# State tiles of four streams in the ring of raw weights, and norm sums with one column, in a one-core encoder kernel

## The chip, the core and the metric

The kernel runs on one core of a Trainium2 chip. Its time is the device time of one execution in microseconds (us); lower is better. A core has TensorE (PE; its weight loads are listed as PEld), VectorE (DVE), ScalarE (ACT), GpSimd (POOL) and SyncE (SP). All transfers of this kernel are issued from SP, in order, and run on 16 DMA engines.

## What is computed

The reference is one inference step of a layer with two mixers and an MLP, on 2048 prompt frames with 16 meta tokens ahead of them, and on 8 running streams of 16 frames each. Cut to what matters here:

```python
def rms_norm(x, g):                      # also: layer norm over the conv channels
    return x * rsqrt(mean(x * x) + EPS) * g

def retention_block(q, k, v, S):         # one chunk; S is the carried state, 128 x 128 a head
    scores = einsum('bihd,bjhd->bhij', q, k) * d_intra
    intra = einsum('bhij,bjhe->bihe', scores, v)
    inter = einsum('bihd,bhde->bihe', q, S) * d_in
    S_new = S * exp(lg * L) + einsum('bjhd,bjhe,hj->bhde', k, v, d_out)
    return intra + inter, S_new

q, k, v, gate, u = mixer_inputs(x, pos, g_pre, w_in)     # rms_norm, one projection, rotary q and k
ret = retention over chunks, conv = depthwise conv + layer norm + swish
x = x + rms_norm(concat(ret * swish(gate), conv) @ w_out)
x = x + rms_norm(relu(rms_norm(x) @ w_mlp_in) ** 2 @ w_mlp_out)
```

There are 4 heads of 128. Each of the 8 streams has a state of 128 x 128 per head, which is read, used by `inter`, updated and written back.

## The kernel before

The tokens are cut into six groups; a group is three blocks of 128 tokens, or two blocks and the 8 x 16 tokens of the streams. Group 0 also holds the meta tokens; group 3 (`SG`) holds the streams. Tokens lie in the columns of most tiles.

The first stage (up to about 1000 us) runs over the groups. For a group it normalizes x (`norm_group`), projects it with weight units of 128 x 1024 (`proj`, `values`), runs the convolution of the group on VectorE (L780), the retention of each head (`head_tail`), and one group later the output projection (`out_units`). The second stage is the MLP. Products with weights are made from operands split in a high and a low part, so each takes three matmuls (L459 to L461; L878 to L880 for values).

Weights come in through `fetch`. A unit that is met for the first time is loaded unsplit into two tiles of 128 x 512 named `raw` (a ring of five, `RB[0]`), and split by ScalarE and GpSimd (L260, L261); the split parts are saved, and from then on they are loaded in split form (`whi`, `wlo`, a ring of nine, L236 and L237). The last weight that is split before the MLP is one of `out_units` of group 1, so from then on the ring of `raw` stands idle until the first stage ends.

**A head's tail.** `head_tail` is a generator; each `yield` lets other work in. Its first step transposes k (`tk`) and makes the scores (`sc`, then `sd` on VectorE). Its second step (from L949) computes the prompt's state updates (`up`, `S`), and for group 3 the streams. For the streams, GpSimd has laid out the queries in `qdm` so that a matmul with the state of stream s reaches the columns of s only. In two rounds of four streams it makes `us` (k times v per stream, from keys masked in `ks` by VectorE and GpSimd), then twice for two streams: load the states into `sst` (L983), add their `inter` part to `os` (L985), update the states on VectorE (L987) and store them (L989). `sst` is a ring of two tiles, each for two streams. The third step makes `ob`, then for each block the mean and variance (`bn_stats`, L1001 and L1002), a reciprocal root in eight small VectorE instructions, and `on` on ScalarE (L1012), which `ot` transposes (L1017).

**Sums for norms.** `rstd_bcast` gets a tile of squares `acc`, summed over all but the partitions. It sums over the partitions with a matmul per block of 128 tokens, in which the squares are the weights and a 128 x 128 tile of ones is streamed (L432, result `st`). All 128 columns of the result are equal; column 0 is read. Then come the root, a diagonal matrix `dg` of it per block (L436), and a matmul with ones that spreads it over the partitions (`rb`, L440). It is called for the norm of each group, for the layer norm of each group's convolution (`conv_norm`, whose mean is `mu`, L799) and twice each for groups 1 and 2 ahead of the MLP (`mlp_in`).

**What sets the order.** The code is not run in the order of its text: a scheduler with a model of the times lays out each engine's instructions (`schedule_with_timeline_sim=True`), under the priorities that generators get in `advance`. A tile of a ring is reused once its last reader is done. So an edit at one place can change the order on every engine.

Of the kernel before, what the change touches and what calls it, by code (L numbers as in the profile page):

```python
# [12 lines left out]
F32 = mybir.dt.float32  # L13
# [3 lines left out]
ALU = mybir.AluOpType  # L17
# [3 lines left out]
P = 128  # L21
D_MODEL, SEQ, N_META, PAST_LEN = 1024, 2048, 16, 512
NS, SL = 8, 16
# [31 lines left out]
def _log_gamma():  # L55
    return np.log1p(-np.exp2(np.float32(-5.0) - np.arange(NH, dtype=np.float32))).astype(np.float32).astype(np.float64)
# [95 lines left out]
def build(nc, T):  # L152
    lg = _log_gamma()
    with tile.TileContext(nc, schedule_with_timeline_sim=True) as tc, ExitStack() as top:
# [26 lines left out]
        ones = cst[:, CC["ones"]:CC["ones"] + P]  # L181
# [37 lines left out]
        rawps, RB = [], [5]  # L219
# [190 lines left out]
        def rsqrt_small(ss, nb, n):  # L410
            return rsqrt(ss, n, *(spool.tile([P, 4], F32, tag=f"nw{i}", name=f"nw{i}")[:, :nb] for i in range(5)))
# [12 lines left out]
        def rstd_bcast(acc, W, n):  # L424

            starts = list(range(0, W - P + 1, P))
            if starts[-1] + P < W:
                starts.append(W - P)
            nb = len(starts)
            ps = auxp.tile([P, 4, P], F32, tag="aux", name="st")  # L430
            for b, s in enumerate(starts):
                nc.tensor.matmul(ps[:, b, :], acc[:, s:s + P], ones, start=True, stop=True)  # L432
            y = rsqrt_small(ps[:, :nb, 0], nb, n)
            dg = spool.tile([P, NM // P, P], F32, tag="dg", name="dg", bufs=1)
            for b in range(nb):
                nc.vector.tensor_scalar(out=dg[:, b, :], in0=ident, scalar1=y[:, b:b + 1], scalar2=None, op0=ALU.mult)  # L436
            yield WAIT
            rb = auxp.tile([P, 512], F32, tag="aux", name="rb")
            for b, s in enumerate(starts):
                nc.tensor.matmul(rb[:, s:s + P], ones, dg[:, b, :], start=True, stop=True)  # L440
            return rb[:, :W]
# [39 lines left out]
        def mlp_in(gi):  # L481
# [27 lines left out]
            def norm(acc):  # L509
                if early:  # L510
                    rb = yield from rstd_bcast(acc, N, D_MODEL)
                    rs = tp.tile([P, WM], F32, tag="rs", name="rs", bufs=1)[:, :N]
                    nc.scalar.activation(out=rs, in_=rb, func=AF.Copy)
                    return rs
                sb = np_.tile([P, WM], F32, tag="acc", name="acc")[:, :N]
                nc.scalar.activation(out=sb, in_=acc, func=AF.Copy)
                yield WAIT
                return (yield from rstd_wide(sb, N, D_MODEL))
# [114 lines left out]
        tp = em(tc.tile_pool(name="tp", bufs=2))  # L633
# [15 lines left out]
        qdm = stp.tile([P, NS * P], F32, name="qdm")  # L649
# [3 lines left out]
        def norm_group(gi):  # L653
# [27 lines left out]
            for k in range(KT):  # L681
                add_square(acc[:, :W], xk[k], k, W, eng=nc.gpsimd if gi == 1 else None)
                yield
            yield WAIT
            rb = yield from rstd_bcast(acc[:, :W], W, D_MODEL)
            if gi == 0:
                rs = tp.tile([P, WM], F32, tag="rs", name="rs", bufs=1)
# [102 lines left out]
        def conv_norm(gi):  # L790
            N = LAY[gi]["N"]
            z = [zs[gi, c] for c in range(4)]
            acc = np_.tile([P, WM], F32, tag="acc", name="cacc")[:, :N]
            nc.vector.tensor_tensor(out=acc, in0=z[0][:, :N], in1=z[1][:, :N], op=ALU.add)
            nc.vector.tensor_tensor(out=acc, in0=acc, in1=z[2][:, :N], op=ALU.add)
            nc.vector.tensor_tensor(out=acc, in0=acc, in1=z[3][:, :N], op=ALU.add)
            yield WAIT
            mu = auxp.tile([P, 512], F32, tag="aux", name="mu")
            nc.tensor.matmul(mu[:, :N], ones, acc, start=True, stop=True)  # L799
            acc2 = np_.tile([P, WM], F32, tag="acc", name="cacc2")[:, :N]  # L800
            for c in range(4):
                nc.vector.scalar_tensor_tensor(out=z[c][:, :N], in0=mu[:, :N], scalar=-1.0 / (4 * P),
                                               in1=z[c][:, :N], op0=ALU.mult, op1=ALU.add)
                add_square(acc2, z[c][:, :N], c, N, 4 * P)
            yield WAIT
            rb = yield from rstd_bcast(acc2, N, 4 * P)
            for c in range(4):
                nc.vector.tensor_tensor(out=z[c][:, :N], in0=z[c][:, :N], in1=rb, op=ALU.mult)
                sg = tp.tile([P, WM], F32, tag="sg", name="csg")
                nc.scalar.activation(out=sg[:, :N], in_=z[c][:, :N], func=AF.Sigmoid, scale=pcol("cln_g", c),  # L810
                                     bias=pcol("cln_b", c))
                nc.vector.tensor_scalar(out=z[c][:, :N], in0=z[c][:, :N], scalar1=pcol("cln_g", c),
                                        scalar2=pcol("cln_b", c), op0=ALU.mult, op1=ALU.add)
                e1 = nc.vector if c < 3 else nc.gpsimd
                e1.tensor_tensor(out=z[c][:, :N], in0=z[c][:, :N], in1=sg[:, :N], op=ALU.mult)
                split(z[c][:, :N], cats[gi][0][:, 4 + c, :N], cats[gi][1][:, 4 + c, :N])
                yield
            normed.add(gi)
# [85 lines left out]
        def head_tail(gi, h, kr, qr, vf):  # L904
            g = LAY[gi]
            m, N, nb, smp = g["meta"], g["N"], g["nb"], g["smp"]
            nt = nb + smp
            blk = [slice(b * P, (b + 1) * P) for b in range(nt)]
            sblk = slice(nb * P, N)

            tk = auxp.tile([P, 512], F32, tag="aux", name="tk")
            tv = auxp.tile([P, 512], F32, tag="aux", name="tv") if m else None
# [19 lines left out]
            for b in range(nt):  # L932
# [5 lines left out]
                                    in1=dmask[:, h, :].unsqueeze(1).to_broadcast([P, nt, P]), op=ALU.mult)  # L938
            nc.gpsimd.tensor_tensor(out=v3(qd, nb), in0=v3(qr, nb),
                                    in1=din[:, h, :].unsqueeze(1).to_broadcast([P, nb, P]), op=ALU.mult)  # L940
            if smp:
# [3 lines left out]
                                        in0=qr[:, sblk].rearrange("p (s x) -> p s x", s=NS),  # L945
                                        in1=din[:, h, :SL].unsqueeze(1).to_broadcast([P, NS, SL]), op=ALU.mult)
# [11 lines left out]
            for b in range(nb):  # L958
# [3 lines left out]
                else:  # L962
                    sn = stp.tile([P, P], F32, tag=f"S{h}", name=f"S{h}", bufs=2)
                nc.vector.scalar_tensor_tensor(out=sn, in0=S[h], scalar=float(np.exp(lg[h] * P)), in1=up[:, blk[b]],
                                               op0=ALU.mult, op1=ALU.add)
# [3 lines left out]
            if smp:  # L969
                osm = auxp.tile([P, 512], F32, tag="aux", name="os")[:, :P]  # L970
                for s0 in range(0, NS, 4):
                    us = auxp.tile([P, 4, P], F32, tag="aux", name="us")
                    for s in (s0, s0 + 2):
                        ks = tp.tile([P, 2, P], F32, tag="ks", name="ks")
                        eng = nc.vector if s % 4 < 1 else nc.gpsimd
                        eng.tensor_tensor(out=ks, in0=kd[:, sblk].unsqueeze(1).to_broadcast([P, 2, P]),
                                          in1=smask[:, s:s + 2].unsqueeze(2).to_broadcast([P, 2, P]), op=ALU.mult)
                        for i in range(2):
                            nc.tensor.matmul(us[:, s - s0 + i], ks[:, i], vt[:, sblk], start=True, stop=True)
                    for s1 in (0, 2):  # L980
                        s = s0 + s1
                        sst = tp.tile([P, 2, P], F32, tag="sst", name="sst", bufs=2)
                        nc.sync.dma_start(sst, T["state"][h][:, s:s + 2, :])  # L983
                        for i in range(2):
                            nc.tensor.matmul(osm, qdm[:, (s + i) * (P - SL):(s + i) * (P - SL) + P], sst[:, i],  # L985
                                             start=(s + i == 0), stop=False)
                        nc.vector.scalar_tensor_tensor(out=sst, in0=sst, scalar=float(np.exp(lg[h] * SL)),  # L987
                                                       in1=us[:, s1:s1 + 2], op0=ALU.mult, op1=ALU.add)
                        nc.sync.dma_start(T["o_ss"][h][:, s:s + 2, :], sst)  # L989
                nc.tensor.matmul(osm, sd[:, sblk], vt[:, sblk], start=False, stop=True)  # L990
            yield

# [7 lines left out]
            for b in range(nt):  # L1000
# [7 lines left out]
                                           op1=ALU.mult)  # L1008
# [368 lines left out]
```

## Time and profile before

| what | value |
|---|---|
| median of the 3 runs shown | 2451.93 us |
| range of these runs | 2447.64 to 2454.78 us |
| the profiled execution, its own time | 2451.31 us |
| its span, first to last instruction | 2449.4 us |
| TensorE busy | 2358.0 us (96%) |
| VectorE busy | 1512.6 us (62%) |
| ScalarE / GpSimd busy | 913.3 / 1135.8 us |
| mean granted clock of TensorE | 0.982 |
| HBM | 445.20 MB read, 136.61 MB written |

Busy times are shares of the whole span, over stages with different limits. A matmul's listed duration is its latency; matmuls overlap, so spacing is read from the starts of neighbours. The granted clock is 1 at 2.4 GHz and 0.5 at 1.2 GHz; a value between is a mean over a stretch. A fp32 matmul counts as two passes in the trace, each with a weight load of its own.

### The profile page before, as it was taken

To read this page: it belongs to the slowest core of one execution; us is meant where nothing else is said; L and a number is where in the kernel's file an instruction comes from. 1 tells how busy PE (TensorE), PEld (TensorE's weight loads), DVE (VectorE), ACT (ScalarE), POOL (GpSimd) and SP (SyncE) were. 2 spreads that over 40 slices of the span, in tenths; PEclk is the share of its full clock that TensorE was granted. 3 is DMA by queue.
4 is the path that set the end of the run, shared out by engine and by line. 5 is a ranking of instruction groups with operands and counts; after the bars stand their busy time and mean duration, and the time that the engine had idled before them with its cause. 6 is when DMAs were issued, how large, how long until landed. Compare 5 with 4: busy or idle time off the path is not lost.

```text
span 2449.4 us, 40812 instructions
## 1 busy us (share of the span) xinstructions
PE 2358.0 (96%) x14538; PEld 2328.0 (95%) x14538; DVE 1512.6 (62%) x3320; ACT 913.3 (37%) x1928; POOL 1135.8 (46%) x1028
## 2 busy tenths in 40 slices
PE   7999999997999998899999999999999999999997
PEld 7898999997999998899999999999999999999996
DVE  8999896996987956456643347465433375333335
ACT  5544334133233234444444444333222353333332
POOL 6846232132132115778797785333522355332333
PEclk9999999998999999899999999999999999999998
DMA  8887787897687779658796567676854477555552
GB/s 312 294 312 274 258 293 253 253 346 255 202 299 256 251 238 351 217 204 306 268 325 206 185 226 234 233 232 225 287 168 148 157 235 252 181 175 187 179 183 86
DMA packets 246332, 584.53 MB, mean 239 GB/s; under 512 B 31984, under 2 KB 106480, under 8 KB 246128
## 3 DMA queue, kind: packets, MB, share of 16 engines
q1 hardware_dynamic: 246128, 581.92, 70.1%
q8 instruction: 115, 1.88, 0.3%
q14 instruction: 89, 0.73, 0.1%
HBM read 445.20 MB, written 136.61 MB: 238 GB/s over the span
## 4 chain that ended last, share of the span: by engine, by line
PE 71%; DVE 13%; DMA 9%; issue 3%; POOL 2%; ACT 1%; SPq 0%; DVEq 0%; POOLq 0%; ACTq 0%
PE mm L1171 8%; PE mm L1172 7%; PE mm L1173 7%; PE mm L459 5%; PE mm L461 5%; PE mm L460 5%; PE mma L459 4%; PE mma L460 4%; PE mma L461 4%; PE mmc L460 4%; PE mmc L461 4%; PE mmc L459 4%; DVE cv L780 4%; DMA s<-yscr 3%; PE mm L878 1%
## 5 line engine op out<-in xcount | busy, mean ns | idle before, releaser
L261 POOL TENSOR_TENSOR wlo<-raw,whi 128x512 fp32r<-128x512 f32 x276 | 362.7, 1334 | 283.1 <-PE mma L461 113.2
L1173 PE MATMUL mm<-op,wp 128*128 128x384 f32 (+1 forms) x1344 | 440.4, 329 | 4.6 <-POOL wp L300 4.5
L1172 PE MATMUL mm<-op,wp 128*128 128x384 f32 (+1 forms) x1344 | 441.7, 329 | 2.7 <-DVE op L329 2.7
L1171 PE MATMUL mm<-op,wp 128*128 128x384 f32 (+1 forms) x1344 | 438.9, 329 | 4.7 <-DMA wp<-wprod 2.3
L780 DVE SCALAR_TENSOR_TENSOR cv<-ext,par,cv 128x384 f32<-128x384 f32 (+1 forms) x720 | 381.4, 569 | 2.0
L459 PE MATMUL mm<-hhi,whi 128*128 128x384 f32 (+2 forms) x992 | 333.5, 336 | 18.5 <-ACT whi L260 7.0
L461 PE MATMUL mm<-hhi,wlo 128*128 128x384 f32 (+2 forms) x992 | 332.0, 336 | 5.9 <-DVE wlo L261 2.7
L460 PE MATMUL mm<-hlo,whi 128*128 128x384 f32 (+2 forms) x992 | 331.5, 335 | 0.3
L1233 DVE TENSOR_TENSOR ya<-mmc,ya 128x384 f32<-128x384 f32 (+1 forms) x344 | 182.3, 535 | 210.2 <-PE mmc L461 208.8
L1233 DVE TENSOR_TENSOR ya<-mma,ya 128x384 f32<-128x384 f32 (+1 forms) x344 | 182.8, 534 | 197.5 <-PE mma L461 196.7
L329 POOL TENSOR_TENSOR fl<-c,fh 128x384 fp32r<-128x384 f32 (+1 forms) x144 | 142.4, 989 | 335.8 <-ACT fh L328 306.2
L459 PE MATMUL mma<-fh,whi 128*128 128x384 f32 (+1 forms) x768 | 254.1, 332 | 6.9 <-DVE ya L1233 5.8
L1171 PEld LDWEIGHTS mm<-op,wp 128*128 128x128 f32 x1344 | 253.4, 189 | 7.7 <-DMA wp<-wprod 3.5
L1173 PEld LDWEIGHTS mm<-op,wp 128*128 128x128 f32 x1344 | 254.1, 189 | 5.4 <-POOL wp L300 5.2
L1172 PEld LDWEIGHTS mm<-op,wp 128*128 128x128 f32 x1344 | 254.1, 189 | 3.8 <-DVE op L329 3.3
L459 PE MATMUL mmc<-fh,whi 128*128 128x384 f32 (+1 forms) x768 | 251.1, 328 | 2.6 <-ACT fh L328 2.6
L460 PE MATMUL mma<-fl,whi 128*128 128x384 f32 (+1 forms) x768 | 251.7, 328 | 0.8 <-POOL fl L329 0.8
L460 PE MATMUL mmc<-fl,whi 128*128 128x384 f32 (+1 forms) x768 | 251.8, 328 | 0.6 <-POOL fl L329 0.6
L461 PE MATMUL mmc<-fh,wlo 128*128 128x384 f32 (+1 forms) x768 | 251.2, 328 | 1.0 <-POOL wlo L261 1.0
L461 PE MATMUL mma<-fh,wlo 128*128 128x384 f32 (+1 forms) x768 | 251.7, 328 | 0.4 <-POOL wlo L261 0.4
L260 ACT ACTIVATE whi<-raw 128x512 fp32r<-128x512 f32 x288 | 167.7, 623 | 153.0 <-PE mm L1173 83.1
L459 PEld LDWEIGHTS mm<-hhi,whi 128*128 128x128 f32 x992 | 191.8, 193 | 21.3 <-ACT whi L260 8.2
(234 smaller groups left out, 4872.2 us busy)
## 6 DMA issues: line engine op xcount, KB each, us to landing
wp<-wprod SPq DMA_DIRECT2D x224, 512.0 KB, 4.1
raw<-w SPq DMA_DIRECT2D x256, 256.0 KB, 3.8
wprod<-wp SPq DMA_DIRECT2D x112, 512.0 KB, 3.8
whi<-wkeep_in SPq DMA_DIRECT2D x108, 512.0 KB, 6.3
wlo<-wkeep_in SPq DMA_DIRECT2D x108, 512.0 KB, 5.4
raw<-w_in SPq DMA_DIRECT2D x72, 256.0 KB, 5.4
whi<-wkeep_out SPq DMA_DIRECT2D x36, 512.0 KB, 6.3
wlo<-wkeep_out SPq DMA_DIRECT2D x36, 512.0 KB, 5.6
```

The costliest lines, as they stand in the source:

```text
L260: nc.scalar.activation(out=hi[:, c], in_=raw, func=AF.Copy)
L261: (nc.vector if i < 24 and i % 4 == 0 else nc.gpsimd).tensor_tensor(out=lo[:, c], in0=raw, in1=hi[:, c].bitcast(F32), op=ALU.subtract)
L329: (eng or nc.gpsimd).tensor_tensor(out=lo, in0=src, in1=hi.bitcast(F32), op=ALU.subtract)
L459: nc.tensor.matmul(ps, whi(k), ahi(k), start=(k == 0), stop=False)
L460: nc.tensor.matmul(ps, whi(k), alo(k), start=False, stop=False)
L461: nc.tensor.matmul(ps, wlo(k), ahi(k), start=False, stop=(k == nk - 1))
L780: nc.vector.scalar_tensor_tensor(out=o, in0=src(t), scalar=wt, in1=o, op0=ALU.mult, op1=ALU.add)
L878: nc.tensor.matmul(o, hhi[:, k, c], whi, start=(k == 0), stop=False)
L1171: nc.tensor.matmul(ps, hi, ops[:, k, :n], start=start, stop=False, skip_group_check=not first)
L1172: nc.tensor.matmul(ps, hi, ops[:, 4 + k, :n], start=False, stop=False, skip_group_check=not first)
L1173: nc.tensor.matmul(ps, lo, ops[:, k, :n], start=False, stop=(k == 3), skip_group_check=not first)
L1233: last_y[0] = nc.vector.tensor_tensor(out=y, in0=ps, in1=y, op=ALU.add)
```

## The change

Two edits. First, `head_tail` of group 3 takes two tiles from the ring of `raw` at its start, each for four streams, and issues their loads there; four streams are then used, updated by one VectorE instruction and stored by one transfer. Second, the sums over the partitions in `rstd_bcast` stream one column of ones and write one column.

```diff
@@ rstd_bcast
-                nc.tensor.matmul(ps[:, b, :], acc[:, s:s + P], ones, start=True, stop=True)
+                nc.tensor.matmul(ps[:, b, :1], acc[:, s:s + P], ones[:, :1], start=True, stop=True)
@@ head_tail, start
+            ssts = []
+            for s0 in range(0, NS if smp else 0, 4):
+
+                ssts.append(rawps[0].tile([P, 512], F32, tag="raw", name="sst", bufs=RB[0]).rearrange(
+                    "p (s d) -> p s d", s=4))
+                nc.sync.dma_start(ssts[-1], T["state"][h][:, s0:s0 + 4, :])
@@ head_tail, streams
-                    for s1 in (0, 2):
-                        s = s0 + s1
-                        sst = tp.tile([P, 2, P], F32, tag="sst", name="sst", bufs=2)
-                        nc.sync.dma_start(sst, T["state"][h][:, s:s + 2, :])
-                        for i in range(2):
-                            nc.tensor.matmul(osm, qdm[:, (s + i) * (P - SL):(s + i) * (P - SL) + P], sst[:, i],
-                                             start=(s + i == 0), stop=False)
-                        nc.vector.scalar_tensor_tensor(out=sst, in0=sst, scalar=float(np.exp(lg[h] * SL)),
-                                                       in1=us[:, s1:s1 + 2], op0=ALU.mult, op1=ALU.add)
-                        nc.sync.dma_start(T["o_ss"][h][:, s:s + 2, :], sst)
+                    sst = ssts[s0 // 4]
+                    for i in range(4):
+                        nc.tensor.matmul(osm, qdm[:, (s0 + i) * (P - SL):(s0 + i) * (P - SL) + P], sst[:, i],
+                                         start=(s0 + i == 0), stop=False)
+                    nc.vector.scalar_tensor_tensor(out=sst, in0=sst, scalar=float(np.exp(lg[h] * SL)), in1=us,
+                                                   op0=ALU.mult, op1=ALU.add)
+                    nc.sync.dma_start(T["o_ss"][h][:, s0:s0 + 4, :], sst)
```

In the changed kernel, lines behind `head_tail`'s start have numbers six higher, and lines behind the streams' part three higher (the loads are L915, `os` L988, the store L992, `ot` L1020).

Where instructions now stand, at two places. Row texts are those of the schedule: line, operation, tile<-tiles, shape, and the semaphores that the row waits for (DMAHW are those of transfers).

The transfer queue (SP) in head 1 of group 3, before: stores of the first two `sst` tiles (6873, 6879), and behind them the loads of the next two (6894, 6900).

```order
L537 DMA hd0_108<-s_6816 128x384 [waits DMAHW4_49,DVE_49]
L989 DMA o_ss<-sst_6873 128x256 [waits DMAHW5_49,DVE_49]
L989 DMA o_ss<-sst_6879 128x256 [waits DMAHW6_49,DVE_49]
L537 DMA hd0_108<-s_6921 128x384 [waits DMAHW7_49,DVE_49]
L237 DMA wlo_7479<-wkeep_in_96 128x1024 [waits DMAHW0_49,PE_49]
L236 DMA whi_7559<-wkeep_in_96 128x1024 [waits DMAHW1_49,PE_49]
L983 DMA sst_6894<-state 128x256 [waits DMAHW5_49,DMAHW2_49]
L983 DMA sst_6900<-state 128x256 [waits DMAHW6_49,DMAHW3_49]
L237 DMA wlo_7560<-wkeep_in_96 128x1024 [waits DMAHW4_49,PE_49]
L236 DMA whi_7602<-wkeep_in_96 128x1024 [waits PE_49]
```

SP in the changed kernel, during `out_units` of group 1: the first three of eight state loads (6055 and 6057 for head 0, 6779 for head 1), between the last `raw` loads and saves of split weights.

```order
L259 DMA raw_4531<-w_out 128x512 [waits DMAHW0_49,Pool_49]
L322 DMA wkeep_out_97<-wlo_4294 128x1024 [waits DMAHW1_49,Pool_49]
L915 DMA sst_6055<-state 128x512 [waits DMAHW2_49]
L237 DMA wlo_4380<-wkeep_out_97 128x1024 [waits DMAHW3_49,PE_49]
L1042 DMA yscr1_100<-yo_4266 128x384 [waits DMAHW4_49,Activation_49]
L320 DMA wkeep_out_97<-whi_4429 128x1024 [waits DMAHW5_49,Activation_49]
L236 DMA whi_4489<-wkeep_out_97 128x1024 [waits DMAHW6_49,PE_49]
L1042 DMA yscr1_100<-yo_4330 128x384 [waits DMAHW7_49,Activation_49]
L915 DMA sst_6057<-state 128x512 [waits DMAHW0_49,Pool_49]
L322 DMA wkeep_out_97<-wlo_4430 128x1024 [waits DMAHW1_49,Pool_49]
L915 DMA sst_6779<-state 128x512 [waits DMAHW2_49]
L237 DMA wlo_4490<-wkeep_out_97 128x1024 [waits DMAHW3_49,PE_49]
```

The fourth and fifth follow within ten rows. The loads moved from group 3 into group 1's output projection, two groups earlier; the sixth to eighth stand in group 3, each behind the store that frees its tile. The last of them, for head 3 (7348), stands as follows in head 1 of group 3, behind the store of 6779:

```order
L992 DMA o_ss<-sst_6779 128x512 [waits DMAHW6_49,DVE_49]
L537 DMA hd0_108<-s_6743 128x384 [waits DMAHW7_49,DVE_49]
L537 DMA hd0_108<-s_6812 128x384 [waits DMAHW0_49,DVE_49]
L992 DMA o_ss<-sst_6781 128x512 [waits DMAHW1_49,DVE_49]
L237 DMA wlo_7368<-wkeep_in_96 128x1024 [waits DMAHW2_49,PE_49]
L236 DMA whi_7446<-wkeep_in_96 128x1024 [waits DMAHW3_49,PE_49]
L537 DMA hd0_108<-s_6905 128x384 [waits DMAHW4_49,DVE_49]
L915 DMA sst_7348<-state 128x512 [waits DMAHW6_49,DMAHW5_49]
L702 DMA cos_7442<-cos 128x384 [waits DVE_49]
```

TensorE (PE) in group 3, before: the end of head 1's streams has just passed; `mu`, `ot` and `st` follow one another, then head 2's `tk` and `sc`, then a projection.

```order
L461 MATMUL mm_7563<-hhi_5346,wlo_7388 128x384
L799 MATMUL mu_7062<-cacc_6991,cst_91 128x384 [waits DVE_49]
L1017 MATMUL ot_7106<-cst_91,on_7058 128x128 [waits Activation_49]
L1017 MATMUL ot_7106<-cst_91,on_7058 128x128
L1017 MATMUL ot_7106<-cst_91,on_7058 128x128 [waits Activation_49]
L432 MATMUL st_7115<-cst_91,cacc2_7064 128x128 [waits DVE_49]
L432 MATMUL st_7115<-cst_91,cacc2_7064 128x128 x2
L914 MATMUL tk_7172<-cst_91,kr_6852 128x128 x3
L933 MATMUL sc_7179<-qr_6957,kr_6852 128x128 [waits Activation_49]
L933 MATMUL sc_7179<-qr_6957,kr_6852 128x128 x2
L459 MATMUL mm_7606<-hhi_5346,whi_7478 128x384 [waits DMAHW0_49,DVE_49]
```

PE in the changed kernel, head 1's streams: both halves of `os` now stand right behind the first `us`.

```order
L985 MATMUL us_6860<-vt_5732,ks_6861 128x128 [waits DVE_49]
L985 MATMUL us_6860<-vt_5732,ks_6861 128x128
L985 MATMUL us_6860<-vt_5732,ks_6865 128x128 [waits Pool_49]
L985 MATMUL us_6860<-vt_5732,ks_6865 128x128
L988 MATMUL os_6859<-sst_6779,qdm_126 128x128 x4
L988 MATMUL os_6859<-sst_6781,qdm_126 128x128 x4
L993 MATMUL os_6859<-vt_5732,sd_6794 128x128 [waits Pool_49]
L460 MATMUL mm_7213<-hlo_3630,whi_6985 128x384
```

`mu` follows 30 rows later, 102 rows earlier than before, and after it 55 projections' matmuls. Then:

```order
L1020 MATMUL ot_7090<-cst_91,on_7042 128x128 [waits Activation_49]
L459 MATMUL mm_7450<-hhi_5346,whi_7284 128x384
L1020 MATMUL ot_7090<-cst_91,on_7042 128x128 [waits Activation_49]
L432 MATMUL st_7099<-cst_91,cacc2_7048 128x1 [waits DVE_49]
L1020 MATMUL ot_7090<-cst_91,on_7042 128x128 [waits Activation_49]
L432 MATMUL st_7099<-cst_91,cacc2_7048 128x1 x2
L920 MATMUL tk_7160<-cst_91,kr_6848 128x128 x3
L460 MATMUL mm_7450<-hlo_5347,whi_7284 128x384
```

Before, nothing stood between `mu` and `ot`, or between `st` and the next projection's wait but head 2's `tk` and `sc`; now projections stand ahead of `ot`, between `tk` and `sc` (20), and behind `sc`.

## Rows read from the trace of the kernel before

**Rows 1.** the page, part 1: busy time of the engines

```profile
PE 2358.0 (96%) x14538; PEld 2328.0 (95%) x14538; DVE 1512.6 (62%) x3320; ACT 913.3 (37%) x1928; POOL 1135.8 (46%) x1028
```

**Rows 2.** the page, part 4: the chain that ended last, by engine

```profile
PE 71%; DVE 13%; DMA 9%; issue 3%; POOL 2%; ACT 1%; SPq 0%; DVEq 0%; POOLq 0%; ACTq 0%
```

**Rows 3.** windows: length, busy PE, PEld, DVE, ACT, POOL, clock, DMA share, GB/s

```profile
500.00:600.00 100.00, 90.47 (x559) 88.41 (x559) 79.91 (x218) 30.28 (x69) 28.72 (x31) 0.93 0.88 306
600.00:700.00 100.00, 93.66 (x601) 92.68 (x600) 94.58 (x223) 26.19 (x58) 22.11 (x23) 0.98 0.69 229
1200.00:1400.00 200.00, 200.00 (x1154) 199.73 (x1153) 82.39 (x151) 85.19 (x163) 164.90 (x139) 1.00 0.70 243
```

**Rows 4.** timeline of PE: start, us, line, tiles, count [idle before <-releaser]

```profile
541.31 0.38 PE L878 MATMUL mm<-whi,hhi 128*128 128x256 f32 x1 [1.86 <-DVE kr L826]
562.88 1.06 PE L985 MATMUL os<-sst,qdm 128*128 128x128 f32 x8
585.01 0.82 PE L1017 MATMUL ot<-cst,on 128*128 128x128 f32 x3 [1.90 <-ACT on L1012]
587.69 1.65 PE L432 MATMUL st<-cst,cacc 128*128 128x128 f32 x6 [1.85 <-DVE cacc L454]
594.50 0.69 PE L459 MATMUL mm<-hhi,whi 128*128 128x384 f32 x1 [3.24 <-DVE gs L898]
603.50 1.16 PE L985 MATMUL os<-sst,qdm 128*128 128x128 f32 x8 [0.51 <-DVE S L964]
605.45 1.13 PE L979 MATMUL us<-vt,ks 128*128 128x128 f32 x8 [0.79 <-DVE z L808]
611.70 1.51 PE L985 MATMUL os<-sst,qdm 128*128 128x128 f32 x8 [4.04 <-DMA sst<-state]
```

**Rows 5.** waits, 480 to 660: total us, times, longest us

```profile
DVE sst L987 <- PE os L985: 10.8, 4, 8.3
PE os L985 <- DMA sst<-state: 5.7, 3, 4.0
```

**Rows 6.** timeline of the transfer queue: start, us, line, transfer

```profile
567.68 1.62 SPq L989 DMA_DIRECT2D o_ss<-sst  x2
573.30 0.81 SPq L983 DMA_DIRECT2D sst<-state  x2
```

**Rows 7.** tile sst: time from issue to landing

```profile
DMA to landing us min/median/max: 2.1/4.2/10.2
```

**Rows 8.** timeline of DVE, 553 to 580

```profile
560.08 0.81 DVE L796 TENSOR_TENSOR cacc<-cacc,z 128x384 f32<-128x384 f32 x1
579.57 0.42 DVE L987 SCALAR_TENSOR_TENSOR sst<-sst,us 128x256 f32<-128x256 f32 x1 [8.28 <-PE os L985]
```

**Rows 9.** windows of 10 us

```profile
580.00:590.00 10.00, 6.25 (x31) 5.19 (x31) 6.14 (x21) 3.36 (x8) 1.76 (x2) 0.77 0.82 283
590.00:600.00 10.00, 6.76 (x26) 6.46 (x26) 7.45 (x23) 6.97 (x16) 1.34 (x2) 0.55 0.36 111
610.00:620.00 10.00, 8.30 (x42) 8.20 (x43) 8.23 (x22) 2.78 (x8) 4.63 (x6) 0.83 0.26 81
```

**Rows 10.** tile st: ns min/median/max, first and last start, forms

```profile
L432 PEld LDWEIGHTS st<-cst,acc x60: 187/192/193, 13.3 to 734.5; 128*128 128x128 f32 x60
L432 PE MATMUL st<-cst,acc x60: 269/275/276, 13.4 to 734.6; 128*128 128x128 f32 x60
L432 PE MATMUL st<-cst,cacc x34: 271/275/580, 173.1 to 905.1; 128*128 128x128 f32 x34
```

**Rows 11.** timeline of PE at 13 us

```profile
13.40 0.83 PE L432 MATMUL st<-cst,acc 128*128 128x128 f32 x6
```

**Rows 12.** timeline of PE at 723 us

```profile
722.74 1.65 PE L953 MATMUL up<-vt,kd 128*128 128x128 f32 x6 [3.35 <-DVE sd L937]
```

**Rows 13.** timeline of PE at 220 us

```profile
219.93 0.54 PE L459 MATMUL mm<-hhi,whi 128*128 128x384 f32 x1 [1.85 <-DMA whi<-wkeep_in]
222.29 0.69 PE L461 MATMUL mm<-hhi,wlo 128*128 128x384 f32 x1 [1.50 <-DMA wlo<-wkeep_in]
```

## The prediction

> **What bounds the kernel now.** I read the page first. TensorE is busy for 96% of the span [rows 1] and 71% of the chain that ended last lies on it [rows 2]. So time comes back in two ways only: TensorE is given less to do, or it waits less. For the waits I went to the stretch that the change touches. The four head tails of group 3 (the group with the stream blocks) run from 498 to 643 us. In the two windows of 100 us there TensorE is idle for 9.5 and 6.3 us, and VectorE is nearly as full as TensorE, above all from 600 to 700 [rows 3]. The timeline of TensorE names the pauses: 1.86 before a value matmul, 1.90 before `ot`, 1.85 before `st`, 3.24 before a gate's projection, 0.51 and 0.79 in head 2's tail and 4.04 before `os` [rows 4].
>
> The list of waits ties them to the state tiles. TensorE waited 5.7 us in three places for a state to land, and VectorE waited 10.8 us in four places for `os`, because its update of a state (L987) stands in its in-order queue until `os` has read that state [rows 5]. The queue of transfers shows why a state is late: the `sst` ring has two tiles, so a load stands behind the store of the tile before it. In head 1 the store is issued at 567.68 and the load at 573.30 [rows 6]; a transfer of `sst` or `o_ss` takes 4.2 us to land in the middle, 10.2 at most [rows 7]. So head 1's second half of `os` runs just ahead of 579.57, where VectorE's wait of 8.28 us for it ends, though the sum that `mu` needs (`cacc`) was done by 560.9 [rows 8]. Behind that wait come the bn statistics, `on` and `ot`, then `mu`, `cacc2`, `st`, and after them the squares and the gate that free the bank for the next projection. These are the pauses from 585 to 605. They also cost clock: the granted clock is 0.77 of full in 580 to 590, 0.55 in 590 to 600 and 0.83 in 610 to 620 [rows 9], that is, after each longer pause TensorE ran for a time at the lower of its levels, 1.2 in place of 2.4 GHz.
>
> **The change, part by part.**
>
> *State loads.* Sixteen loads and sixteen stores of 128 KB become eight and eight of 256 KB; the bytes stay. The queue's rows show five loads issued already among the output weights of group 1, two groups before use; the sixth to eighth wait for the stores of the first to third. Both halves of `os` in head 1 now stand right behind `us`, where the first half ran at 562.88 [rows 4].
>
> - Waits for a state: 5.7 us [rows 5]. I take all of it. Bounds: nothing comes back if the late three loads are again late; at most 5.7.
> - Clock lost behind the 4.04 pause: TensorE was busy 8.30 us of 610 to 620 at 0.83 [rows 9], so 8.30 x 0.17 = 1.4. All of it goes with the pause.
> - The chain behind head 1's late `os`: pauses 1.90 + 1.85 + 3.24 + 0.51 + 0.79 = 8.3 [rows 4], and clock 6.25 x 0.23 + 6.76 x 0.45 = 1.4 + 3.0 = 4.4 [rows 9], together 12.7. The new order has `mu` 102 instructions earlier on TensorE and 55 projections between it and the first `ot`, where none stood before; at 0.173 us each (1154 matmuls of that width fill 200 us of the MLP [rows 3]) this is 9.5 us of cover. Against the whole coming back: the gate's pause comes from a crowd on VectorE, of which the state wait is only a part. I take two thirds, 8.5; bounds 0 and 12.7.
> - VectorE: sixteen updates of 128x256 become eight of 128x512, the same elements with half the starts. Nothing.
> - The 1.86 pause before a value matmul [rows 4] comes from the rotary step and stays.
>
> *Raw ring.* Its five tiles now carry state from the last split weight of group 1 on. Until the MLP no weight is split, so nothing else asks for them. Five times 256 KB more are loaded during group 1's output projection, where TensorE has none of the pauses above. Nothing, while the weights' lead covers it.
>
> *Sums with one column.* 60 + 34 = 94 passes of 128 columns [rows 10] (47 matmuls, two passes each). Six in a row take 0.83 us from the first's start to the last's end, each 0.275 long: (0.83 - 0.275) / 5 = 0.111 us a pass [rows 10, 11]. The trace has no pass with one column. Free passes would save 94 x 0.111 = 10.4; a pass still limited by loading its 128 weight columns saves nothing. Each pass has a load of 0.19 us [rows 10], and nothing in the trace that loads 128 columns follows its forerunner closer than 0.111. That is the nearest row, so I take 1.0; bounds 0 and 10.4, and below 0 under the rivals.
>
> The Trainium skill speaks here against the change: "TensorE: Matmul & The Clock Gate", section "LDWEIGHTS (loading the stationary operand)", has a load take the number of its columns over 1.2 ns, 107 ns for 128; by that an estimate of the saving is 94 x 0.004 = 0.4 us. The same page's section "Back-to-back issue gap" has a matmul of 1 to 64 columns follow after 25 ns; by that it would be 94 x 0.086 = 8 us. The trace can't part the two, since streaming 128 columns in two steps each takes the same 0.111.
>
> *A new order.* The scheduler lays out the stage up to about 1000 us anew on every engine; the MLP's rows read almost as before. Other small pauses will be hit or missed, each of the size of the ones seen (0.5 to 1.9). I charge 2 us.
>
> Sum: 5.7 + 1.4 + 8.5 + 1.0 - 2 = 14.6. The profiled execution took 2451.3 us (span 2449.4), 0.6 under the median of the runs shown, 2451.9, so either may be the base. 2451.3 - 14.6 = 2436.7: I predict **2437 us**. A measurement of this kernel can tell about 0.3%, 7.4 us, from no change.
>
> **The rivals.**
>
> 1. *VectorE was the bound there anyway.* TensorE arrives earlier and waits for VectorE instead. For: VectorE is busy 94.6 of 100 us from 600 to 700 [rows 3]; the pause before `up` at 722.74 (3.35, for `sd` of VectorE) is of that kind [rows 12], and the new order has the same pattern there. Against: VectorE gets back its own 10.8 us of waits. Then about half of the first three terms stays, 7.8 - 2 + 1 = 6.8, less a pause like 3.35: 2445 to 2450.
> 2. *Weights come late.* The queue of transfers is in order; the late loads stand in it until stores land, and weights stand behind them. That is what the pauses of 1.85 and 1.50 at 219.93 and 222.29 look like [rows 13], with 1.4 to 3.0 of lost clock behind such pauses [rows 9]: 5 us a time. Three would eat the gain: 2451. Against: a weight is asked for three units ahead, 3 x 24 matmuls x 0.173 = 12 us, and a store lands in about 4 [rows 7].
> 3. *Slower: loads that nothing hides.* With one column nothing streams while the next weights load. If each pass then paid its load and its own latency in full, 0.19 + 0.275 = 0.467 in place of 0.111 [rows 10, 11], that is 94 x 0.356 = 33 us. The rest gives 13.6, so 2471. It comes out slower by more than 0.3% from a spacing of 0.111 + (13.6 + 7.4) / 94 = 0.334 us a pass. Against: loads run ahead of the passes everywhere else (0.19 long at a spacing of 0.111).
> 4. *The loads are not early.* The queue's rows exclude this for five of eight.
>
> **How the numbers follow.** Forecast 0.70 (2427 to 2444: the chain term from 1 to its bound of 12.7, the sums from 0 to some 8); rival 1 0.14; rival 2 0.08, of which 0.02 ends slower; rival 3 0.08. So faster 0.70, same 0.20 (0.14 + 0.06), slower 0.10. The range goes from 2427 to 2452, which takes in rivals 1 and 2; rival 3 and a gain above 24 us stay outside.
>
> **What would show it.** Right: in group 3 no wait of TensorE for `sst`, VectorE's wait for `os` under 3 us in all, no granted clock under 0.9 in the windows that answer to 580 to 620, TensorE's idle time there (15.8 us in 500 to 700) down to about 5. For the sums: the spacing of the one-column passes; 0.1 confirms the load as limit, 0.03 would add 7 us of gain. Wrong: the pauses come back under other names between 560 and 730, weights named as releasers at 320 to 360 or 560 to 620, or `st` passes over 0.2 apart.

## The result, and the profile after

The changed kernel takes 2424.22 us (median of 4 runs, 2420.58 to 2427.17), the kernel before 2453.36 in runs beside it: a ratio of 0.9881 (95% interval 0.9869 to 0.9893), 29.1 us less. The forecast was 14.6 less, 2437, and the range ended at 2427. The direction was right, the size half of what came. The profiled execution of the changed kernel took 2426.03 us, 25.2 less by its span.

The page, part 1 [rows 1]:

```profile
PE 2346.8 (97%) x14538; PEld 2319.5 (96%) x14538; DVE 1507.9 (62%) x3312; ACT 913.9 (38%) x1928; POOL 1138.5 (47%) x1028
```

TensorE does the same 14538 passes in 11.2 us less busy time (a pass at the lower clock is busy for longer), and the rest of the gain, 14.0 us of the span, is idle time. The windows that answer to [rows 3] and, in tens, to [rows 9], in the same columns:

```profile
500.00:600.00 100.00, 96.98 (x642) 95.26 (x641) 91.78 (x238) 38.67 (x86) 37.52 (x38) 1.00 0.91 322
600.00:700.00 100.00, 100.00 (x645) 99.93 (x644) 93.69 (x228) 24.81 (x56) 24.04 (x25) 1.00 0.78 265
...
580.00:590.00 10.00, 10.00 (x68) 10.00 (x67) 10.00 (x27) 6.28 (x15) 3.29 (x3) 1.00 0.82 271
590.00:600.00 10.00, 8.34 (x62) 8.12 (x61) 10.00 (x15) 6.24 (x14) 6.48 (x6) 1.00 0.62 201
```

Idle time of TensorE in 500 to 700 went from 15.8 to 3.0 us, and no window is below full clock. VectorE is fuller than before from 500 to 600 (91.8 against 79.9 us) and about as full after it, yet between 494 and 678 us TensorE's waits for it come to 2.9 us in place of 8.3. The timeline of TensorE, where [rows 4] were:

```profile
558.98 1.95 PE L988 MATMUL os<-sst,qdm 128*128 128x128 f32 x16
560.77 0.39 PE L993 MATMUL os<-vt,sd 128*128 128x128 f32 x2
...
566.61 0.81 PE L799 MATMUL mu<-cacc,cst 128*128 128x384 f32 x2
...
576.78 0.27 PE L1020 MATMUL ot<-cst,on 128*128 128x128 f32 x1
...
577.17 0.28 PE L432 MATMUL st<-cst,cacc 128*128 128x1 f32 x2
...
596.73 0.55 PE L920 MATMUL tk<-cst,kr 128*128 128x128 f32 x3 [1.66 <-DVE sst L990]
```

All of head 1's `os` is done by 561.2; `mu` comes at 566.61 (582.30 before), and `ot` and `st` follow 10 us later with projections between and no pause. All that TensorE waited for in group 3 (494 to 678 us):

```profile
PE tk L920 <- DVE sst L990: 1.7, 1, 1.7
PE ob L998 <- DVE sst L990: 0.7, 1, 0.7
PE rb L440 <- DVE dg L436: 0.5, 1, 0.5
```

The two new waits are for the update of a state (L990), which now takes 683 ns in one piece. The queue's row shows the loads of the states:

```profile
L915 SPq DMA_DIRECT2D sst<-state x8: 332/424/773, 327.5 to 568.0; - x8
L990 DVE SCALAR_TENSOR_TENSOR sst<-sst,us x8: 672/683/689, 509.4 to 620.1; 128x512 f32<-128x512 f32 x8
```

**Where the gain lies.** Four marks on TensorE cut the trace: `tk` of head 0 in group 3, the first `tk` of group 4, the last `mu` (the convolution of the last group), and the first `sw` (a norm inside the MLP). Before:

```profile
493.32 0.49 PE L914 MATMUL tk<-cst,kr 128*128 128x128 f32 x3
697.84 0.49 PE L914 MATMUL tk<-cst,kr 128*128 128x128 f32 x3
895.74 0.81 PE L799 MATMUL mu<-cacc,cst 128*128 128x384 f32 x2
1085.33 0.81 PE L418 MATMUL sw<-acc,cst 128*128 128x384 f32 x2
```

After:

```profile
494.40 0.49 PE L920 MATMUL tk<-cst,kr 128*128 128x128 f32 x3
678.03 0.49 PE L920 MATMUL tk<-cst,kr 128*128 128x128 f32 x3
873.73 0.81 PE L799 MATMUL mu<-cacc,cst 128*128 128x384 f32 x2
1056.81 0.81 PE L418 MATMUL sw<-acc,cst 128*128 128x384 f32 x2
```

Group 3 went from 204.5 to 183.6 us (20.9 less), groups 4 and 5 from 197.9 to 195.7, the entry of the MLP from 189.6 to 183.1 (6.5 less), a stretch that neither edit touches. What comes ahead costs 1.1 more and the rest of the MLP some 3 more. So two things had to be explained: why group 3 gave more than the 15.6 forecast for it, and why the MLP's entry gave anything.

### The profile page after: what moved, and what is told of

Same layout as the page of the kernel before. It is cut to its first block, busy times and chain, and to the rows that moved or that the text cites. A ratio compares the mean times of both kernels' runs of the same rounds, so it can differ in the third digit from the quotient of the medians.

```text
span 2424.2 us, 40779 instructions
## 1 busy us (share of the span) xinstructions
PE 2346.8 (97%) x14538; PEld 2319.5 (96%) x14538; DVE 1507.9 (62%) x3312; ACT 913.9 (38%) x1928; POOL 1138.5 (47%) x1028
## 4 chain that ended last, share of the span: by engine, by line
PE 72%; DVE 10%; DMA 10%; POOL 3%; issue 2%; ACT 1%; SPq 1%; DVEq 0%; POOLq 0%; ACTq 0%
PE mm L1174 7%; PE mm L1175 7%; PE mm L1176 7%; PE mm L461 6%; PE mm L460 6%; PE mm L459 6%; PE mmc L460 4%; PE mma L459 4%; PE mmc L461 4%; PE mma L460 4%; PE mmc L459 4%; PE mma L461 4%; DVE cv L780 3%; DMA s<-yscr 3%; DMA st<-hd 2%
## 5 line engine op out<-in xcount | busy, mean ns | idle before, releaser
L1236 DVE TENSOR_TENSOR ya<-mma,ya 128x384 f32<-128x384 f32 (+1 forms) x344 | 182.9, 534 | 196.5 <-PE mma L461 195.7
```

Of the source, the lines that this page charges most:

```text
L1236: last_y[0] = nc.vector.tensor_tensor(out=y, in0=ps, in1=y, op=ALU.add)
```

## The experiments

Three theories. **A**: a state that is there when `os` wants it gives back its wait and the whole chain behind it; that is the gain in group 3. **C**: the one-column sums give some 10 us. **B**, later sharpened to **L**: part of the gain comes from the layout, not from the states' times. The state tiles left the pool `tp`, which became 2 KB a partition smaller; when the MLP's pools are laid over the first stage's, other tiles come to lie on each other (read from the code; no run shows the addresses).

All eleven kernels by the marks of their own traces (one profiled execution each, so good to a few us; the ratios are from the timed runs; the trace with `tp` as large as before is of the longest of its six executions, 2440.84 us against a median of 2432.95, and it reaches group 3 some 4 us later than the changed kernel's):

| kernel | ratio to before | group 3 | groups 4, 5 | MLP's entry |
|---|---|---|---|---|
| before | 1 | 204.5 | 197.9 | 189.6 |
| changed | 0.9881 (0.9869 to 0.9893) | 183.6 | 195.7 | 183.1 |
| states alone | 0.9865 (0.9852 to 0.9879) | 185.1 | 195.7 | 179.5 |
| sums alone | 1.000 (0.9987 to 1.0013) | 205.6 | 195.1 | 191.4 |
| one late tile of four | 0.9951 (0.9935 to 0.9967) | 213.1 | 184.2 | 179.4 |
| two tiles of four | 0.9868 (0.985 to 0.9886) | 183.3 | 194.7 | 180.1 |
| changed, `tp` as large as before | 0.992 (0.9905 to 0.9935) | 184.4 | 198.2 | 190.2 |
| before, `tp` smaller | 0.9963 (0.995 to 0.9976) | 204.3 | 198.2 | 181.4 |
| updates in pairs | 0.9877 (0.9862 to 0.9892) | 184.0 | 194.8 | 181.2 |
| `stq` ahead of `x1p` | 0.9966 (0.9953 to 0.9979) | 185.5 | 197.1 | 198.8 |
| `stq` of four tiles | 0.9882 (0.9861 to 0.9904) | 183.4 | 196.2 | 182.9 |

**1. The states alone** (the change without its second edit):

```diff
-                nc.tensor.matmul(ps[:, b, :1], acc[:, s:s + P], ones[:, :1], start=True, stop=True)
+                nc.tensor.matmul(ps[:, b, :], acc[:, s:s + P], ones, start=True, stop=True)
```

> The state part of the change alone: states of four streams early in the raw ring, the sums with 128 columns as before. Its laid-out order is nearly that of the changed kernel. Theory A (the states and the chain behind them give the gain; one column saves (0.111 - 0.094) x 94 = 1.6 us at most): 2424 to 2427. Theory C (the one-column sums give some 10 us of it): 2432 to 2435. Theory B (part of the gain is the new order): 2424 to 2427 too, since the order is kept.

Measured: 2422.05. The first edit brings the whole gain. It makes the states early and `tp` smaller at once; runs 5 and 6 part the two.

**2. The sums alone** (the kernel before with the second edit).

> The sums part alone: one column streamed and written in rstd_bcast, the states in pairs in a ring of two as before. Its laid-out order is nearly that of the kernel before. Theory A: 2450 to 2453 (0 to 1.6 us gained, group 3 with its waits for sst, the MLP's entry as before). Theory C: 2443. If the one-column sums bring the shorter entry of the MLP, the stretch from 900 to 1060 us is some 9 us shorter here.

Measured: 2453.87 against 2453.46. Theory C falls: one column brings nothing, within 0.13%. Group 3 and the MLP's entry are as before.

**3. One late tile.** All states go through one tile of four streams, so a load stands behind the store of the round before (the loads at the head's start are gone):

```diff
-                    sst = ssts[s0 // 4]
+                    if not held:
+                        held.append(rawps[0].tile([P, 512], F32, tag="raw", name="sst", bufs=RB[0]).rearrange(
+                            "p (s d) -> p s d", s=4))
+                    sst = held[0]
+                    nc.sync.dma_start(sst, T["state"][h][:, s0:s0 + 4, :])
```

> The changed kernel, but all states go through one tile of four streams, loaded in the round that uses it, so that each load stands behind the store of the round before, as in a ring of two pairs. Theory A: the waits for sst come back and with them the chain in group 3: 15 to 25 us lost there, 2440 to 2450. Theory B (the gain comes from the new order and from the fewer, larger instructions): 2424 to 2432, the waits for sst covered by other work. The MLP's entry tells whether its 9 us hang on early states.

Measured: 2440.52, as theory A has it. Groups 3 to 5 together take 397.2 us, against 379.3 in the changed kernel: 18 us that come with late states. (The two are taken together, since group 3 is longer here than before the change and groups 4 and 5 shorter.) What TensorE waited for in group 3 is the lesson of this run:

```profile
PE sc L934 <- ACT rn L1021: 4.8, 1, 4.8
PE ot L1019 <- ACT on L1014: 3.9, 1, 3.9
PE rb L440 <- DVE dg L436: 2.7, 1, 2.7
...
PE os L987 <- DMA sst<-state: 1.1, 1, 1.1
```

and VectorE, in the same stretch:

```profile
DVE sst L989 <- PE os L987: 8.3, 2, 7.8
```

The wait that names the state is 1.1 us. The other 11.4 listed here are under the names of ScalarE and VectorE: VectorE's queue holds an update that waits for `os`, and ScalarE's `on` behind it waited for VectorE's `nm`. That each of these waits goes back to a late state is read from the order of the queues; no run parts them. The MLP's entry is short here too, though the states are late: it doesn't hang on them.

**4. Two tiles of four**, held for the whole group, loaded a head ahead:

```diff
-                ssts.append(rawps[0].tile([P, 512], F32, tag="raw", name="sst", bufs=RB[0]).rearrange(
-                    "p (s d) -> p s d", s=4))
+                if len(held) < 2:
+                    held.append(rawps[0].tile([P, 512], F32, tag="raw", name="sst", bufs=RB[0]).rearrange(
+                        "p (s d) -> p s d", s=4))
+                ssts.append(held[(2 * h + s0 // 4) % 2])
```

> The changed kernel, but with two fixed tiles of four streams in place of the ring of five: the loads of a head stand behind the stores of the head before it, some 25 us before their use. Theory A (a state must be there when os wants it, and no earlier): 2422 to 2428, no wait of TensorE for sst. If the depth of five is what counts: 2432 or more, with waits for sst in group 3.

Measured: 2423.63. A ring of two tiles of four does all that the ring of five does: heads 1 to 3 are loaded within group 3, so loads two groups ahead are not needed for them.

**5. The changed kernel with `tp` as large as before.** An unused tile takes the place that the states had left:

```diff
+            if smp and h == 0:
+                pad = tp.tile([P, 2, P], F32, tag="pad", name="pad", bufs=2)
+                nc.gpsimd.memset(pad[:, 0, :1], 0.0)
```

> The changed kernel, with an unused tile of 2 KB a partition put into the pool that the pairs of states had left, so that this pool is as large as before; states early as in the change. Laid out so, the transfers at the MLP's entry stand in the order of before again. Theory L (some 6 to 10 us of the gain come from the smaller pool, because the MLP's tiles that are loaded first lie over the tiles of the first stage): from the last mu to the first sw 189 to 192 us in place of 179 to 183, 2430 to 2434 in all; group 3 as fast as in the changed kernel (20 us ahead of before at head 0's tk of group 4). Theory A alone (all of the gain is early states): 2421 to 2426.

Measured: 2432.95; the entry is 190.2, group 3 stays at 184.4. Theory L holds. What TensorE waited for between the last `mu` and the first `sw` (longest rows; `wp` is a part of an MLP weight made from `raw`, `op` and `chi` are parts of split operands), here:

```profile
PE mm L1179 <- POOL wp L300: 3.3, 2, 2.7
PE mm L461 <- DMA wlo<-wkeep_out: 3.0, 2, 2.5
PE mm L1178 <- DVE op L329: 2.4, 2, 1.8
```

in the kernel before:

```profile
PE mm L1173 <- POOL wp L300: 4.5, 1, 4.5
PE mm L461 <- DMA wlo<-wkeep_out: 3.9, 1, 3.9
PE mm L1172 <- DVE op L329: 2.7, 2, 1.9
```

and in the changed kernel:

```profile
PE mm L459 <- ACT chi L328: 3.8, 2, 3.5
PE mm L461 <- DMA wlo<-wkeep_out: 2.8, 1, 2.8
PE mm L1176 <- POOL wp L300: 1.5, 1, 1.5
```

The pad brings back the waits of before, line by line (L1173 and L1179 are the same line). The queue of transfers shows another order as well. With the pad the MLP's raw weights come one, then three (L282; the tiles into which h is loaded, L561, are called `st` as well):

```profile
917.96 0.33 SPq L282 DMA_DIRECT2D raw<-w  x1
...
930.94 2.96 SPq L282 DMA_DIRECT2D raw<-w  x3
```

as in the kernel before:

```profile
932.12 0.33 SPq L282 DMA_DIRECT2D raw<-w  x1
...
946.51 2.89 SPq L282 DMA_DIRECT2D raw<-w  x3
```

and in the changed kernel two, behind seven loads of h:

```profile
901.96 14.96 SPq L561 DMA_DIRECT2D st<-hd  x7
917.02 0.85 SPq L282 DMA_DIRECT2D raw<-w  x2
```

**6. The kernel before with the smaller `tp`.** Its two tiles of two streams are the halves of one raw tile, and everything else is as before:

```diff
-                        sst = tp.tile([P, 2, P], F32, tag="sst", name="sst", bufs=2)
+                        if not held:
+                            held.append(rawps[0].tile([P, 512], F32, tag="raw", name="sst", bufs=RB[0]).rearrange(
+                                "p (s d) -> p s d", s=4))
+                        sst = held[0][:, s1:s1 + 2]
```

> The kernel before, with its two state tiles of two streams cut from one tile of the raw ring: the rhythm of loads, updates and stores as before, only the pool of the stage's tiles is 2 KB smaller. Theory L: group 3 as slow as before, the MLP's entry 6 to 10 us shorter, 2443 to 2447. Theory A alone: 2450 to 2455.

Measured: 2442.91. Group 3 is as slow as before, the entry as short as after, with the changed kernel's longest waits there (`wlo` 3.1, `chi` 2.9, `wp` 1.5 us) and its order of transfers (two raw weights behind seven loads of h). With run 5 this closes a square: early states alone give 0.80%, the layout alone 0.37%, together 1.17%; both at once measured 1.19%. Of 2453.4 us that is 19.6 and 9.1. Within the intervals, which are 0.13 to 0.15% either way, the two gains are separate and add up (run 5 has the one-column sums as well, which run 2 puts at nothing).

**7. Updates and stores in pairs**, states early:

```diff
-                    nc.vector.scalar_tensor_tensor(out=sst, in0=sst, scalar=float(np.exp(lg[h] * SL)), in1=us,
-                                                   op0=ALU.mult, op1=ALU.add)
-                    nc.sync.dma_start(T["o_ss"][h][:, s0:s0 + 4, :], sst)
+                    for s1 in (0, 2):
+                        nc.vector.scalar_tensor_tensor(out=sst[:, s1:s1 + 2], in0=sst[:, s1:s1 + 2],
+                                                       scalar=float(np.exp(lg[h] * SL)), in1=us[:, s1:s1 + 2],
+                                                       op0=ALU.mult, op1=ALU.add)
+                        nc.sync.dma_start(T["o_ss"][h][:, s0 + s1:s0 + s1 + 2, :], sst[:, s1:s1 + 2])
```

> The changed kernel, states loaded early and four at a time, but updated by VectorE and stored in pairs as before (sixteen updates and stores in place of eight). Theory A (early is what counts): 2421 to 2427. If the larger updates and stores bring part of it: 2428 or more, with waits for sst's updates in group 3.

Measured: 2424.87. Larger updates and stores are worth nothing that this can tell (0.15% either way).

**8. Another layout of the MLP**, tried for a faster version:

```diff
         fp = ep(tc.tile_pool(name="fp", bufs=2))
+        stqs.append(ep(tc.tile_pool(name="stq", bufs=3)))
         x1p = ep(tc.tile_pool(name="x1p", bufs=1))
         rawps.append(x1p)
         RB.append(8)
-        stqs.append(ep(tc.tile_pool(name="stq", bufs=3)))
```

> The changed kernel, with the MLP's pool of tiles for its loads of h (stq) opened ahead of the pool that holds its raw weights (x1p), so that the raw weights lie over space that is free earlier; their first loads then stand ahead of four of the loads of h that they stood behind. Theory L (the layout at the MLP's entry is worth some us either way): the entry from the last mu to the first sw comes to 173 to 179 us, 2416 to 2421. If the raw weights are not what the entry waits for: 2421 to 2428, or slower if the loads of h come late.

Measured: 2445.71, a miss: the raw weights come earlier and the entry is 15.7 us longer. The split operands of the MLP come late instead:

```profile
PE mm L1174 <- ACT op L328: 9.4, 4, 5.3
```

So one order of pools against another moved 9 us in runs 5 and 6 and 21 here, and which tiles have to come first was not foreseen.

**9. A fourth tile for the loads of h** (`bufs=4` for `stq`).

> The changed kernel with a ring of four in place of three tiles for the MLP's loads of h (stq), because in the changed kernel's trace seven such loads hold the queue of transfers for 15.0 us (from 901.96 on) and a weight behind them is 2.8 us late at TensorE. If that hold is what the entry still waits for: no late weight there, the entry from the last mu to the first sw at 174 to 179 us, 2416 to 2421. If the loads only wait elsewhere: 2421 to 2427.

Measured: 2421.41 against 2450.95, the changed kernel's ratio again. The seven loads become six that hold the queue for 12.5 us, and the weight behind them is late all the same (3.6 us in two places). No version was found that beats the changed kernel by more than its interval.

**10. The price of a sum by itself.** Each sum is made five times over, with 1, 64 and 128 columns:

```diff
-                nc.tensor.matmul(ps[:, b, :1], acc[:, s:s + P], ones[:, :1], start=True, stop=True)
+                for _ in range(5):
+                    nc.tensor.matmul(ps[:, b, :64], acc[:, s:s + P], ones[:, :64], start=True, stop=True)
```

> The changed kernel with each sum over the partitions made five times over, one column each (376 passes more, each with its load of 128 weight columns). Theory W (a pass of few columns is limited by the load of its weights, 0.094 us as in the changed kernel's trace): 2424 + 376 x 0.094 = 2459, and 30 passes in a row at 0.09 to 0.10 us each. Theory F (in a long row the one-column passes run faster, the six in a row were still starting up): under 2440, under 0.05 us each.

> The same with 64 columns. Theory W: 0.09 to 0.10 us a pass, as with one column, 2459. If the columns streamed cost as well: 0.10 us or more, 2462.

> The same with 128 columns. Theory W: 0.111 us a pass as before, 2424 + 376 x 0.111 = 2466, so 6 us more than with one column. If in a long row load and columns add up: more than 0.13 us a pass, 2473 or more.

Measured, against 2451.67: 2485.35 with 1 column (ratio 1.013, 1.0106 to 1.0153), 2463.57 with 64 (1.0043, 1.0025 to 1.006), 2459.35 with 128 (1.0027, 1.0009 to 1.0045). One column is the dearest by over 20 us, which no theory had. Rows of 30 passes and the matmul behind them, 1 column:

```profile
320.45 4.17 PE L433 MATMUL st<-cst,acc 128*128 128x1 f32 x30
324.49 0.67 PE L460 MATMUL mm<-hhi,whi 128*128 128x384 f32 x1
...
389.35 3.40 PE L433 MATMUL st<-cst,cacc 128*128 128x1 f32 x30
392.62 0.42 PE L460 MATMUL mm<-hhi,whi 128*128 128x384 f32 x1
```

128 columns:

```profile
382.99 3.51 PE L433 MATMUL st<-cst,cacc 128*128 128x128 f32 x30
386.25 0.42 PE L460 MATMUL mm<-hhi,whi 128*128 128x384 f32 x1
```

From the first start to the start of the next matmul, where that one shows full clock (0.42): 3.27 us for 30 passes of one column, 3.26 of 128, so 0.109 us a pass whatever the columns (3.26 with 64, too). At that price 376 passes more are 41 us; by the ratios, the kernels with 64 and 128 columns are 40 and 36 us over the changed kernel, and the one with 1 column 61. The row at 320.45 took 4.04, and the matmul behind it 0.67 in place of 0.42: the clock had fallen during the row, though TensorE waited for nothing from 300 to 330 us. The windows from 40 to 50 us, in which the second row of sums lies, show the granted clock at 0.66 with 1 column:

```profile
40.00:50.00 10.00, 10.00 (x60) 10.00 (x60) 9.80 (x28) 4.22 (x8) 7.95 (x7) 0.66 0.79 267
```

and at 1.00 with 128:

```profile
40.00:50.00 10.00, 10.00 (x85) 10.00 (x84) 9.80 (x27) 4.95 (x10) 8.66 (x8) 1.00 0.80 276
```

## Why the prediction was wrong, point by point

Two terms of the sum failed: the charge for a new order above all, and the chain behind head 1's late `os`.

**The mechanism in group 3 was right.** The three waits for states are gone, with them VectorE's wait for `os` and the low clocks. Loads start at 327.5 and are early for five of eight, as the queue's rows said; a later ring of two (run 4) would do. VectorE's sixteen updates as eight: nothing, as taken (run 7).

**The chain term was too small.** The smaller of the two steps that failed is "I take two thirds, 8.5; bounds 0 and 12.7", argued with a VectorE that would still be crowded. VectorE is crowded, 91.8 and 93.7 of 100 us, but the 55 projections that now stand between `mu` and `ot` gave TensorE other work, as the order had shown. With the whole bound the terms make 5.7 + 1.4 + 12.7 = 19.8; measured were 20.9 in the two traces and 19.6 by run 5. The 1.86 pause before a value matmul, which was to stay, went too; new waits of 1.7, 0.7 and 0.5 took its place. So the term was missized by 4 to 5 us. With this alone put right the forecast would have been 2432 or 2433, inside the range.

**The charge for a new order had the wrong sign and the wrong cause.** This is the larger step that failed. "I charge 2 us" took the order for chance: small pauses hit or missed. But the diff itself says what moves at a distance: a tag leaves `tp`, the pool shrinks by 2 KB, and tiles of the next stage come to lie elsewhere. That was worth 9.1 us by run 6, so the term was off by 11, and this alone takes the forecast to 2425 or 2426, below the range. With 19.6 for early states and nothing for the sums the gain comes to 28.7; 29.1 was measured. "The MLP's rows read almost as before" was true of the rows and not of its entry. Runs 5 and 6 show that the size of `tp` decides; which tile of the MLP waits for which tile of the first stage wasn't shown, and whether the transfers' order or the tiles' release sets it is open.

**The sums**: 1.0 was taken and 0 came (run 2), with an interval of some 3 us either way that takes in the 1.0. The 0.111 for 128 columns holds: by the same working the long row of 30 gives (3.51 - 0.275) / 29 = 0.112. The 0.094 that the expectations of runs 1 and 10 give a pass of one column doesn't hold. It goes by the modelled end of the last pass; from the first start to the start of the next matmul both widths take the same, here the changed kernel:

```profile
378.08 0.72 PE L432 MATMUL st<-cst,cacc 128*128 128x1 f32 x6
378.67 0.42 PE L459 MATMUL mm<-hhi,whi 128*128 128x384 f32 x1
```

and with 128 columns (run 1):

```profile
376.35 0.83 PE L432 MATMUL st<-cst,cacc 128*128 128x128 f32 x6
376.93 0.42 PE L461 MATMUL mm<-hhi,wlo 128*128 128x384 f32 x1
```

0.59 and 0.58 us for six. That fits a load of 128 columns per pass as the limit, as the choice near 0.111 had it; no run varied the width of the load, so it isn't shown against some other floor per pass. The Trainium skill ("TensorE: Matmul & The Clock Gate", section "LDWEIGHTS (loading the stationary operand)") has a load take its columns over 1.2 in ns, 107 for 128. The 0.109 us measured in long rows agrees. In its section "Back-to-back issue gap" the Trainium skill gives the 25 ns for an isolated matmul, and has the load and the matmul both set the spacing in a stream of such pairs. The prediction's 8 us used the isolated figure; no spacing of 25 ns appears here, where each pass loads weights of its own.

**The rivals.** VectorE as the bound: no; beside the 2.9 us in group 3, only the pause before `up` is left of it [rows 12], 2.79 us in place of 3.35:

```profile
703.93 0.94 PE L959 MATMUL up<-vt,kd 128*128 128x128 f32 x6 [2.79 <-DVE sd L943]
```

Late weights: TensorE waited for none from 320 to 360 or from 560 to 620. Loads that nothing hides: no pass came near 0.334 us, so that rival fell; but in rows five times as long the one-column sums do make the kernel slower than 128 columns do (2485.35 against 2459.35), and TensorE's busy time, part of it at the lower clock, is 32 us longer. With the three blocks of this kernel (six passes) the matmul behind the row above shows full clock (0.42).

## What to carry to other kernels

Price a late transfer by all that stands behind its reader in the in-order queues, not by the wait that names it: in run 3 the named wait was 1.1 us, and groups 3 to 5 were 18 longer. When an edit takes a tile out of a pool, look at the pools that are opened later in that space: 2 KB moved 9 us in a stage that the edit never touched, and an unused tile of the same size tells the two causes apart in one run. Narrowing a matmul's moving side saved nothing here, where each pass loads 128 weight columns; read spacings from start to start.

## What was not expected of the hardware

- A pass that loads 128 weight columns takes 0.109 us with 1, 64 or 128 columns streamed (30 in a row, at full clock).
- Rows of 30 one-column passes lowered TensorE's clock though it issued without a pause: behind eight of the sixteen rows of that run the next matmul ran at the level of 1.2 GHz (0.67 us against 0.42 for 384 columns), behind none of the sixteen with 128 columns. Why the narrower matmuls do this is open. The busy time of TensorE in the whole trace was 2410.6 and 2378.1, 32 us more with the narrower matmuls.
- An unused tile of 2 KB a partition cost 9 to 10 us (0.992 against 0.9881). That it does so through where other tiles come to lie is argued from the waits and the order of transfers, not shown tile by tile.
